# Stick-breaking attention, router constant, convolution taps and chunk scores of a two-layer decoder trunk in another order

## The chip, the core and the metric

The kernel runs on one core of one Trainium2 chip. A core has five engines with queues of their own: TensorE (PE, with its weight loads shown as PEld), VectorE (DVE), ScalarE (ACT), GpSimd (POOL) and SyncE (SP, which here only starts DMA transfers). An engine works through its queue in order and waits on semaphores of the others. The metric is the device time of one execution in microseconds (us); less is better.

## The reference, cut to what matters

Two layers over 256 tokens of width 1024, in fp32. Each layer is a mixer and a mixture of experts; a router common to both layers picks the experts. Layer 0's mixer runs a causal convolution of 31 taps (512 channels) beside stick-breaking attention (8 heads of 64); layer 1's runs chunked gated linear attention (4 heads) beside a pooling mixer.

```python
# stick_breaking_attention, for each block of 128 queries and the keys up to it
z = einsum('bhqd,bhkd->bhqk', q[:, :, start:end], k[:, :, :end])
strict = s_pos < t_pos
log_keep = where(strict, log_sigmoid(-z), 0.0)
later = cumsum(log_keep, axis=3, reverse=True) - log_keep
a = where(strict, exp(log_sigmoid(z) + later), 0.0)
outs.append(einsum('bhqk,bhkd->bhqd', a, v[:, :, :end]))
# gla_chunked
scores = where(causal, einsum('nbhid,nbhjd->nbhij', q_in, k_in), 0.0)
# before each mixture of experts
h = rmsnorm(x, norm_ffn[l]) * (1.0 + sc2) + sh2
scores = softmax(h @ router_w)
```

The router's logits are taken apart: `h @ router_w` is the token's norm times a product with `rwg` = router_w · norm_ffn · (1 + sc2), plus a row of 16 numbers that no token changes, sh2 @ router_w. That row is the **router's constant** `rc`.

## The kernel before, in words

Everything on the chip stays channel by token or token by channel in tiles of 128 partitions; weights come from HBM in a ring of 1 MB buffers, started by SP in program order as buffers come free. In the mixers each weight piece is split in two parts of reduced precision (`g`: L55 on ACT, L56 on DVE) and multiplied by both parts of the activations. The Python code is the order: each engine's queue holds its instructions in the order in which the code issues them, and generators (`next`, `conv`, `fill`) lay small pieces of one job between those of another.

**Layer 0, projections (56 to 105 us).** Five projections `pj` (L418, L423) of 512 columns each; the last three carry the convolution between their pieces by `conv(1 + k % 2, 1 + k % 2)`: so many taps of two generators.

- `taps` (L548) is DVE's share: 59 taps on `yc`, each `yc[k] += yp[k] shifted · weight` (L553; the first of a block L550). It takes channel block 2 (taps 0 to 15), then all 31 of block 0, then 12 of block 1.
- `other_taps` (L558) is the share of ACT and POOL: ACT multiplies (`cv`, L567, three buffers) and POOL adds (L568): block 3 whole, then block 2 from tap 16 on into the same `yc[:, 2]`, then block 1 from tap 12 on into `more`, added at the end (L570).

**Layer 0, attention (105 to 150 us).** Heads go in four pairs `cc`, the two heads of a pair in partitions 0 to 63 and 64 to 127 of `qT` and `kT`. For each pair: `logits` (L608, PE) makes z in PSUM, a product of `identb` and `maskb` putting the mask on its two diagonal blocks; `minus` and `softplus` (ACT and DVE, L624 to L634) make zs and ze; `sums` (L641 to L644, PE) the cumulative sums; `weights` (L648, L649 on DVE, the exp L650 on ACT) the attention weights; `attend` (L655, PE) the product with the values; `attended` (L666 ACT, L667 DVE) takes it out. The driver runs logits(0), logits(1), and then, in a loop over cc, sums(cc), logits(cc + 2), softplus(cc + 1), weights(cc), attend(cc). Between them stand taps (`conv(2, 3)`, `conv(3, 2)`) and, on PE, `fill(n)`: n groups of 8 records (`ada`, L190) of the conditioning product, which streams 1 MB tiles and is needed much later.

**Layer 0, output projection (150 to 200 us).** `po` (L453) in two halves, the second in four blocks i of 256 columns; after each, DVE updates `xT` (L481), and `norm.logits(i - 1)` (`lg`, L293) gives the router's logits of that block. Before the second half stands `Norm.weights` (L370): `gain` (L367), `rwg` (L374), the eight products of `rc` (L377) and its copy to SBUF. Layer 1 does the same (at 530 us).

**Layer 1's mixer (460 to 545 us).** Its projections are again pieces of `pj` on PE, between which steps of a generator lay the gated linear attention: `gs` (L923) are the scores within chunks, for row half q = 0, then 1; `kv` (L938) the products of keys and values.

**Experts (200 to 460 and 560 to 789 us).** Per expert `u`, `g` (L1252) and `dn` (L1285) from weights that stream through the same ring.

## Time and profile before

| what | value |
|---|---|
| median of 3 runs | 794.8 us (791.4, 794.8, 4035.95) |
| the profiled execution | 791.18 us, span 789.5 us |
| busy: PE, DVE, ACT, POOL | 93%, 40%, 30%, 15% of the span |
| mean granted TensorE clock | 0.977 |
| from HBM | 280.59 MB, 357 GB/s over the span |
| longest groups on PE | u and g (L1252) 225.7 us, dn (L1285) 101.7 us, pj 112.7 us, ada 52.0 us, po 51.1 us |

Times in the rows are us from the start of the span. A granted clock of 1.00 is TensorE's upper level of 2.4 GHz, 0.50 the lower of 1.2 GHz. The span says what can be won inside the program; 1.7 us of the profiled execution lie around it.

### The profile page before, as it was taken

The page shows a single profiled execution, that of the slowest core. Times are in us where ns is not written, and L with a number is a line of the kernel's source. Part 1 is how long each engine was busy: PE and PEld are TensorE (multiplying, and loading weights), DVE is VectorE, ACT ScalarE, POOL GpSimd, SP SyncE. Part 2 cuts the span into 40 slices and gives each one's busy share as a digit, 9 for nine tenths or more (in the row PEclk, how much of TensorE's full clock was granted, in tenths as well). Part 3 has the DMA queues.
Part 4 walks back from the last instruction along what each step waited for, and adds up shares of the span by engine and source line. Part 5 has one row for each costly group of instructions (what it writes and reads, how often), then busy time and mean ns, then how long its engine had stood idle before and what let it go on. Part 6 is the DMA issues. An engine that isn't in the chain of part 4 may idle for free. (4 is left out here: it accounts for less than half of the span.)

```text
span 789.5 us, 10674 instructions
## 1 busy us (share of the span) xinstructions
PE 730.9 (93%) x4173; PEld 402.8 (51%) x4173; DVE 313.8 (40%) x563; ACT 235.1 (30%) x441; POOL 120.0 (15%) x168
## 2 busy tenths in 40 slices
PE   6798888998899999999797999999999999999985
PEld 4398645486434335343233677579534334434323
DVE  3459968675214113121115655453513123213214
ACT  3357657463102101110113544551402101001012
POOL 1357646222000000000004500010300000000000
PEclk9999999999999999999999999999799999999999
DMA  8999739954999999999999998496699999999992
GB/s 357 386 375 419 291 121 398 372 219 183 351 410 409 409 409 409 409 408 409 409 405 391 396 414 322 171 402 235 255 385 412 408 409 409 409 408 409 408 403 106
DMA packets 74713, 282.46 MB, mean 358 GB/s; under 512 B 5194, under 2 KB 6438, under 8 KB 69530
## 3 DMA queue, kind: packets, MB, share of 16 engines
q1 hardware_dynamic: 73122, 278.68, 89.9%
q0 software_dynamic: 1344, 2.64, 0.9%
q8 instruction: 35, 0.57, 0.3%
q10 hardware_dynamic: 184, 0.34, 0.1%
q14 instruction: 28, 0.23, 0.1%
HBM read 280.59 MB, written 1.05 MB: 357 GB/s over the span
## 5 line engine op out<-in xcount | busy, mean ns | idle before, releaser
L1252 PE MATMUL g<-w,xg 128*64 128x512 f32 x512 | 115.0, 597 | 1.9 <-DMA w<-in_moe_w_gate_dram 1.8
L1252 PE MATMUL u<-w,xg 128*64 128x512 f32 x496 | 110.7, 594 | 2.1 <-DMA w<-in_moe_w_up_dram 2.1
L1285 PE MATMUL dn<-w,at 128*64 128x512 f32 x448 | 101.7, 604 | 8.1 <-ACTq L1383 6.8
L1264 DVE TENSOR_TENSOR act<-sg,u 128x512 f32<-128x512 f32 (+1 forms) x18 | 11.1, 628 | 153.0 <-PE u L1252 153.0
L1252 PEld LDWEIGHTS u<-w,xg 128*64 128x64 f32 x496 | 34.6, 137 | 72.1 <-issue 64.7
L1252 PEld LDWEIGHTS g<-w,xg 128*64 128x64 f32 x512 | 35.1, 137 | 68.6 <-issue 61.2
L56 DVE TENSOR_TENSOR g<-wi,g 128x512 fp32r<-128x512 f32 x72 | 58.1, 816 | 24.8 <-ACT g L55 24.6
L1285 PEld LDWEIGHTS dn<-w,at 128*64 128x64 f32 x448 | 31.1, 138 | 70.8 <-issue 56.8
L423 PE MATMUL pj<-hT,g 128*128 128x256 f32 x480 | 61.4, 285 | 6.0 <-DVE g L56 4.7
L423 PEld LDWEIGHTS pj<-hT,g 128*128 128x128 f32 x480 | 57.8, 188 | 10.0 <-DVE g L56 6.8
L418 PE MATMUL pj<-g,hT 128*128 128x512 f32 x192 | 51.3, 414 | 7.4 <-DVE g L56 3.5
L55 ACT ACTIVATE g<-wi 128x512 fp32r<-128x512 f32 x72 | 44.4, 626 | 39.1 <-PE pj L423 20.2
L190 PE MATMUL ada<-ad,cond 128*32 128x512 f32 x384 | 52.0, 653 | 4.0 <-DMA ad<-in_ada_w_dram 4.0
L453 PE MATMUL po<-cat,g 128*128 128x256 f32 x372 | 51.1, 290 | 2.5 <-ACT gsr L1006 1.7
L453 PEld LDWEIGHTS po<-cat,g 128*128 128x128 f32 x372 | 46.8, 196 | 6.7 <-ACT gsr L1006 2.6
L418 PEld LDWEIGHTS pj<-g,hT 128*128 128x128 f32 x192 | 35.4, 193 | 22.4 <-DVE g L56 6.7
L568 POOL TENSOR_TENSOR yc<-yc,cv 128x256 f32<-128x256 f32 x45 | 38.9, 864 | 22.8 <-ACT cv L567 20.0
L553 DVE SCALAR_TENSOR_TENSOR yc<-yp,epar,yc 128x256 f32<-128x256 f32 x56 | 41.3, 737 | 1.0
L1317 ACT ACTIVATE ys<-y 128x512 fp32r<-128x512 f32 x28 | 16.9, 625 | 67.1 <-DVE y L1307 62.3
L1275 DVE COPY at<-at 128x512 f32<-128x512 f32 x14 | 9.7, 692 | 67.5 <-PE at L1274 65.9
L1311 ACT ACTIVATE y<-dn,cw 128x512 f32<-128x512 f32 x7 | 4.8, 687 | 103.8 <-PE dn L1285 103.8
L1260 ACT ACTIVATE sg<-g 128x512 f32<-128x512 f32 x14 | 8.4, 597 | 89.4 <-PE g L1252 89.4
(385 smaller groups left out, 887.4 us busy)
## 6 DMA issues: line engine op xcount, KB each, us to landing
w<-in_moe_w_gate_dram SPq DMA_DIRECT2D x64, 1024.0 KB, 16.1
w<-in_moe_w_up_dram SPq DMA_DIRECT2D x62, 1024.0 KB, 18.3
w<-in_moe_w_down_dram SPq DMA_DIRECT2D x61, 1024.0 KB, 18.3
ad<-in_ada_w_dram SPq DMA_DIRECT2D x48, 1024.0 KB, 8.7
wi<-in_w_in_even_dram SPq DMA_DIRECT2D x20, 512.0 KB, 12.1
wi<-in_w_in_odd_dram SPq DMA_DIRECT2D x14, 512.0 KB, 12.5
wo<-in_w_out_even_dram SPq DMA_DIRECT2D x4, 1024.0 KB
wo<-in_w_out_odd_dram SPq DMA_DIRECT2D x4, 1024.0 KB, 18.6
```

The lines of the kernel that those rows point to most:

```text
L55: S.activation(g[0], w, AF.Copy)
L56: (eng or V).tensor_tensor(g[1], w, g[0].bitcast(F32), op=OP.subtract)
L190: PE.matmul(acc[32 * j:32 * j + 32, :], lhsT=cond[:, k, :], rhs=w[:, k - (i if n == 2 else 2 * i), c0:c0 + 512], start=i == 0, stop=i == 4 ...
L418: PE.matmul(bs[t], lhsT=self.h[j][:, k, t * 128:(t + 1) * 128], rhs=g[i], start=k == 0 and p == 0, stop=k == 7 and p == 2)
L423: PE.matmul(bs[c // 2][:, (c % 2) * T:(c % 2 + 1) * T], lhsT=g[i][:, c * 128:(c + 1) * 128], rhs=self.h[j][:, k, :], start=k == 0 and c % ...
L453: PE.matmul(self.acc[kd // 2][:, (kd % 2) * T:(kd % 2 + 1) * T], lhsT=block(g[wi], kd % 4), rhs=cats[ci][:, k, :], start=start and kd % 2 ...
L553: V.scalar_tensor_tensor(yc[:, k], yp[:, k, j:j + T], epar[:, k, j:j + 1], yc[:, k], op0=OP.mult, op1=OP.add)
L568: G.tensor_tensor(y, y, p, op=OP.add)
L1252: PE.matmul(b[64 * e:64 * e + 64, :], lhsT=xg[:, k, o + 64 * e:o + 64 * e + 64], rhs=we[:, e, k % 2 * 512:k % 2 * 512 + 512], start=k == 0 ...
L1264: V.tensor_tensor(a[:, n], sg[:, n], ub[:, n], op=OP.mult)
L1285: PE.matmul(bs[h][64 * e:64 * e + 64, :], lhsT=at[k][:, 64 * e:64 * e + 64], rhs=r[:, e], start=k == 0, stop=k == 3)
L1317: S.activation(ys[:, 0, n], y[h], AF.Copy)
```

## The change

- `logits`: the four products of queries and keys of a pair come first, alternating between the heads; the first now covers 256 queries (two products before). The mask comes last, once per head over both diagonal blocks (twice per head before).
- `attend`: the products with the values alternate between the two heads (head 0 whole, then head 1 before).
- `gs`: the products of both row halves alternate in one group of eight (two groups of four before).
- router's constant: DVE multiplies router_w by sh2 (`rk`) and sums the eight values of a partition (`rp`, L379 of the new numbering); one product with `ones` on PE sums over partitions. It is issued behind `norm.logits(0)` of the second half of `po`; the eight products of before (L377) are gone.
- `taps`: DVE's taps go by turns over two lists, block 0, and block 2 followed by block 1; a tap is taken from the longer list.

```diff
--- before.py
+++ after.py
@@ -372,11 +372,17 @@
             self.gain()
             self.w = live.tile([128, 8, E], F32, tag="rwg", name=f"rwg{l}")
             V.tensor_tensor(self.w, rw, self.g[:, :, None].to_broadcast([128, 8, E]), op=OP.mult)
-            b = bank(f"rc{l}")
-            for k in range(8):
-                PE.matmul(b[:, 0:E], lhsT=mod[l][:, 3, k:k + 1].to_broadcast([128, 128]), rhs=rw[:, k, :],
-                          start=k == 0, stop=k == 7)
-            self.c = live.tile([128, E], F32, tag="rc", name=f"rc{l}")
+            by_k = live.tile([128, E, 8], F32, tag="arow", name=f"rk{l}")
+            V.tensor_tensor(by_k.rearrange("p e k -> p k e"), rw, mod[l][:, 3, :, None].to_broadcast([128, 8, E]), op=OP.mult)
+            of_p = live.tile([128, E], F32, tag="ap", name=f"rp{l}")
+            V.tensor_reduce(of_p, by_k, axis=AX.X, op=OP.add)
+            self.of_p = of_p
+
+        def constant(self):
+
+            b = bank(f"rc{self.l}")
+            PE.matmul(b[:, 0:E], lhsT=ones, rhs=self.of_p, start=True, stop=True)
+            self.c = live.tile([128, E], F32, tag="rc", name=f"rc{self.l}")
             S.activation(self.c, b[:, 0:E], AF.Copy)
 
         def shifted(self, k, out, f, eng):
@@ -485,6 +491,8 @@
                     fill(fills[i])
                     if i:
                         norm.logits(i - 1)
+                    if i == 1:
+                        norm.constant()
                     if i == 2:
                         norm.turned(0, self.banks)
             norm.tokens(0)
@@ -546,13 +554,17 @@
 
 
         def taps():
-            for k, n in ((2, 16), (0, 31), (1, 12)):
-                V.tensor_scalar(yc[:, k], yp[:, k, 0:T], epar[:, k, 0:1], epar[:, k, 31:32], op0=OP.mult, op1=OP.add)
-                yield
-                for j in range(1, n):
+
+            sums = [[(2, j) for j in range(16)] + [(1, j) for j in range(12)], [(0, j) for j in range(31)]]
+            while any(sums):
+                sums.sort(key=len)
+                k, j = sums[1].pop(0)
+                if j == 0:
+                    V.tensor_scalar(yc[:, k], yp[:, k, 0:T], epar[:, k, 0:1], epar[:, k, 31:32], op0=OP.mult, op1=OP.add)
+                else:
                     V.scalar_tensor_tensor(yc[:, k], yp[:, k, j:j + T], epar[:, k, j:j + 1], yc[:, k],
                                            op0=OP.mult, op1=OP.add)
-                    yield
+                yield
 
         def other_taps():
             more = pool.tile([128, T], F32, name="more")
@@ -608,14 +620,15 @@
         def logits(cc):
 
             z = zl[cc] = zz.tile([128, 2, 512], F32, tag="zz", name=f"z{cc}")
+            heads = [slice(64 * h2, 64 * h2 + 64) for h2 in range(2)]
+
+            for h2, r in enumerate(heads):
+                PE.matmul(z[:, h2, 0:256], lhsT=kT[r, cc, 0:128], rhs=qT[r, cc, :], start=True, stop=False)
+            for h2, r in enumerate(heads):
+                PE.matmul(z[:, h2, 256:384], lhsT=kT[r, cc, 128:256], rhs=qT[r, cc, 128:256], start=False, stop=False)
             for h2 in range(2):
-                r = slice(64 * h2, 64 * h2 + 64)
-                zh = z[:, h2]
-                PE.matmul(zh[:, 0:128], lhsT=identb, rhs=maskb, start=True, stop=False)
-                PE.matmul(zh[:, 0:128], lhsT=kT[r, cc, 0:128], rhs=qT[r, cc, 0:128], start=False, stop=False)
-                PE.matmul(zh[:, 128:256], lhsT=kT[r, cc, 0:128], rhs=qT[r, cc, 128:256], start=False, stop=False)
-                PE.matmul(zh[:, 256:384], lhsT=identb, rhs=maskb, start=False, stop=False)
-                PE.matmul(zh[:, 256:384], lhsT=kT[r, cc, 128:256], rhs=qT[r, cc, 128:256], start=False, stop=True)
+                PE.matmul(z[:, h2].rearrange("p (a t) -> p a t", a=2)[:, :, 0:128], lhsT=identb,
+                          rhs=maskb[:, None, :].to_broadcast([128, 2, 128]), start=False, stop=True)
 
 
         def minus(cc):
@@ -655,11 +668,12 @@
         def attend(cc):
             ob = zl[cc] = bank(f"att{cc}")
             a = zs[cc]
-            for h2 in range(2):
-                hc = slice((2 * cc + h2) * 64, (2 * cc + h2) * 64 + 64)
-                r = slice(64 * h2, 64 * h2 + 64)
-                PE.matmul(ob[r, 0:256], lhsT=vn[:, 0, hc], rhs=a[:, h2, 0:256], start=True, stop=False)
-                PE.matmul(ob[r, 128:256], lhsT=vn[:, 1, hc], rhs=a[:, h2, 256:384], start=False, stop=True)
+            for t in range(2):
+                for h2 in range(2):
+                    hc = slice((2 * cc + h2) * 64, (2 * cc + h2) * 64 + 64)
+                    r = slice(64 * h2, 64 * h2 + 64)
+                    PE.matmul(ob[r, 128 * t:256], lhsT=vn[:, t, hc], rhs=a[:, h2, 256 * t:256 + 128 * t],
+                              start=t == 0, stop=t == 1)
 
         def attended(cc):
             hi, lo = (c[:, 4 + cc, :] for c in cats)
@@ -914,18 +928,19 @@
             V.tensor_copy(kdn, halves(b))
             yield
 
-            for q in range(2):
-                b = bank(f"gs{q}").rearrange("p (c i) -> p c i", c=4)
-                o = slice(64 * q, 64 * q + 64)
-                for t in range(2):
-                    ts_ = slice(t * 128, t * 128 + 128)
-                    for cc in range(2):
+            bs = [bank(f"gs{q}").rearrange("p (c i) -> p c i", c=4) for q in range(2)]
+            for t in range(2):
+                ts_ = slice(t * 128, t * 128 + 128)
+                for cc in range(2):
+                    for q, b in enumerate(bs):
+                        o = slice(64 * q, 64 * q + 64)
                         PE.matmul(b[:, 2 * t + cc, :], lhsT=kT[o, cc, ts_], rhs=qT[o, cc, ts_], start=True, stop=True)
-                yield
+            yield
+            for q, b in enumerate(bs):
                 for t in range(2):
                     for cc in range(2):
                         V.copy_predicated(sc[:, t, 2 * cc + q], trii, b[:, 2 * t + cc, :])
-            yield
+                yield
             yield
 
             yield
```

**TensorE, the logits of the first head pair**, right behind the last piece of projection 4 (`z_1076`: the pair's PSUM tile). Before:

```order
L614 LDWEIGHTS identb
L614 MATMUL z_1076<-maskb,identb 128x128
L615 MATMUL z_1076<-qT,kT 128x128
L616 MATMUL z_1076<-qT,kT 128x128
L617 LDWEIGHTS identb
L617 MATMUL z_1076<-maskb,identb 128x128
L618 MATMUL z_1076<-qT,kT 128x128
```

These seven rows stand for one head and come again for the other. In the changed kernel the pair is:

```order
L626 MATMUL z_1076<-qT,kT 128x256 x2
L628 MATMUL z_1076<-qT,kT 128x128 x2
L630 LDWEIGHTS identb
L630 MATMUL z_1076<-maskb,identb 128x2x128
L630 LDWEIGHTS identb
L630 MATMUL z_1076<-maskb,identb 128x2x128
```

Fourteen rows became eight instructions, and the products of the two heads now stand next to each other.

**VectorE, the end of projection 4**: `g038` and `g039` are its last two weight pieces, `ze0` the first step of attention there. Before:

```order
L56 TENSOR_TENSOR g038_1014<-wi20484_981,g038_1014 128x512 [waits DMAHW1_49,Activation_49]
L553 SCALAR_TENSOR_TENSOR yc_276<-yp_153,epar_146,yc_276 128x256 [waits DVE_49]
L56 TENSOR_TENSOR g039_1027<-wi20484_981,g039_1027 128x512 [waits Activation_49]
L553 SCALAR_TENSOR_TENSOR yc_276<-yp_153,epar_146,yc_276 128x256 [waits DVE_49] x7
L626 SCALAR_TENSOR_TENSOR ze0_1114<-zs0_1112 128x768 [waits Activation_49]
```

And in the changed kernel:

```order
L56 TENSOR_TENSOR g038_1014<-wi20484_981,g038_1014 128x512 [waits DMAHW1_49,Activation_49]
L565 SCALAR_TENSOR_TENSOR yc_276<-yp_153,epar_146,yc_276 128x256
L56 TENSOR_TENSOR g039_1027<-wi20484_981,g039_1027 128x512 [waits Activation_49]
L565 SCALAR_TENSOR_TENSOR yc_276<-yp_153,epar_146,yc_276 128x256 [waits DVE_49]
L565 SCALAR_TENSOR_TENSOR yc_276<-yp_153,epar_146,yc_276 128x256
L565 SCALAR_TENSOR_TENSOR yc_276<-yp_153,epar_146,yc_276 128x256 [waits Pool_49]
L565 SCALAR_TENSOR_TENSOR yc_276<-yp_153,epar_146,yc_276 128x256 [waits DVE_49] x2
L563 TENSOR_SCALAR yc_276<-yp_153,epar_146 128x256
L565 SCALAR_TENSOR_TENSOR yc_276<-yp_153,epar_146,yc_276 128x256 [waits DVE_49]
L639 SCALAR_TENSOR_TENSOR ze0_1106<-zs0_1104 128x768 [waits Activation_49]
```

The number of taps is the same; a tap behind one of the other block has no wait for DVE itself, and the last tap of block 2 now stands here, behind a wait for POOL. POOL's first three additions into block 2 (`cv216` to `cv218`) are now these rows of its queue:

```order
L580 TENSOR_TENSOR yc_276<-yc_276,cv216_1038 128x256 [waits DVE_49,Activation_49]
L580 TENSOR_TENSOR yc_276<-yc_276,cv217_1041 128x256 [waits Activation_49,Pool_49]
L580 TENSOR_TENSOR yc_276<-yc_276,cv218_1051 128x256 [waits DVE_49,Activation_49]
```

The first waits for DVE's tap 14 of block 2, which now is the 33rd of DVE's 59 taps (before, block 2's sixteen came first of all); the third waits for tap 15, the last of block 2.

**TensorE, the router's constant of layer 0** (`po`: output projection, `acol`: a piece of the conditioning product). Before:

```order
L199 MATMUL acol_1624<-ident,arow_1444 128x128 x4
L377 MATMUL rc_1635<-rw,mod_148 128x16 x8
L453 MATMUL po_1450<-cat_1074,g_1551 128x256
L453 MATMUL po_1450<-cat_1075,g_1551 128x256
L453 MATMUL po_1450<-cat_1074,g_1551 128x256
```

In the changed kernel:

```order
L190 MATMUL ada_1651<-ad_1687,cond 32x512 x4
L293 MATMUL lg_1693<-rwg_1617,xT 128x16 x4
L384 MATMUL rc_1698<-rp_1621,ones 128x16
L459 MATMUL po_1436<-cat_1074,g_1595 128x256
L459 MATMUL po_1436<-cat_1075,g_1595 128x256
```

The eight products ahead of the second half of the output projection have become one, two blocks later; layer 1's rows read the same.

## Rows read from the trace of the kernel before

**Rows 1.** Busy time by stretch: us of each engine, PE clock, DMA share, GB/s.

```profile
106.00:138.00 32.00, 30.00 (x194) 16.59 (x195) 22.52 (x33) 23.29 (x43) 18.90 (x22) 0.95 0.78 306
460.00:545.00 85.00, 83.30 (x598) 63.19 (x597) 43.42 (x88) 39.43 (x84) 5.20 (x7) 1.00 0.85 328
...
183.00:190.00 7.00, 6.99 (x59) 6.90 (x58) 2.02 (x9) 1.04 (x3) 0.00 (x0) 0.95 0.05 17
```

**Rows 2.** Timeline of PE, one head's logits; columns start us, us, engine, line.

```profile
107.19 0.23 PE L614 MATMUL z<-maskb,identb 128*128 128x128 bf16 x1
107.35 0.49 PE L615 MATMUL z<-qT,kT 64*128 64x128 f32 x2
108.00 0.23 PE L617 MATMUL z<-maskb,identb 128*128 128x128 bf16 x1
108.57 0.23 PE L614 MATMUL z<-maskb,identb 128*128 128x128 bf16 x1
```

**Rows 3.** Busy time of two stretches, and PE's timeline, ada.

```profile
110.80:114.20 3.40, 3.40 (x16) 1.13 (x19) 2.40 (x5) 2.98 (x5) 0.64 (x1) 0.50 0.02 5
138.10:141.50 3.40, 3.40 (x14) 0.90 (x14) 3.29 (x6) 1.74 (x5) 3.08 (x5) 0.50 0.93 318
...
111.68 4.87 PE L190 MATMUL ada<-ad,cond 128*32 128x512 f32 x32
...
133.49 1.92 PE L190 MATMUL ada<-ad,cond 128*32 128x512 f32 x16
```

**Rows 4.** Timeline of PE, products of half the rows or columns.

```profile
122.05 0.66 PE L661 MATMUL att<-zs,vn 128*64 128x256 f32 x4
122.53 0.40 PE L662 MATMUL att<-zs,vn 128*64 128x128 f32 x4
...
481.25 1.16 PE L923 MATMUL gs<-gqT,gkT 64*128 64x128 f32 x8
...
491.97 1.09 PE L938 MATMUL kv<-gvn,gkdn 64*64 64x128 f32 x24
```

**Rows 5.** Page, DVE's taps; timelines of DVE, POOL and ACT, end of projection 4.

```profile
L553 DVE SCALAR_TENSOR_TENSOR yc<-yp,epar,yc 128x256 f32<-128x256 f32 x56 | 41.3, 737 | 1.0
...
101.29 1.21 DVE L56 TENSOR_TENSOR g<-wi,g 128x512 fp32r<-128x512 f32 x1
102.82 0.68 DVE L56 TENSOR_TENSOR g<-wi,g 128x512 fp32r<-128x512 f32 x1
...
93.35 8.60 POOL L568 TENSOR_TENSOR yc<-yc,cv 128x256 f32<-128x256 f32 x9
...
104.49 1.29 ACT L601 ACTIVATE vn<-pj 128x512 f32<-128x512 f32 x2 [4.89 <-PE pj L418]
```

**Rows 6.** Timelines of DVE, PE and ACT, the attention's steps.

```profile
112.36 0.96 DVE L634 SCALAR_TENSOR_TENSOR ze<-zs,ze 128x768 f32<-128x768 f32 x1 [0.96 <-ACT ze L631]
...
116.48 0.70 PE L641 MATMUL zc<-ze,later 128*128 128x256 f32 x2
...
119.56 0.84 ACT L650 ACTIVATE zs<-zs 128x768 f32<-128x768 f32 x1 [2.73 <-DVE zs L649]
128.29 0.84 ACT L650 ACTIVATE zs<-zs 128x768 f32<-128x768 f32 x1 [0.59 <-DVE zs L649]
...
130.27 0.66 PE L661 MATMUL att<-zs,vn 128*64 128x256 f32 x4
...
137.41 0.66 PE L661 MATMUL att<-zs,vn 128*64 128x256 f32 x4 [2.00 <-ACT zs L650]
```

**Rows 7.** Timelines of PE and DVE, the router's constant.

```profile
166.58 1.86 PE L377 MATMUL rc<-rw,mod 128*128 128x16 f32 x16
168.29 3.60 PE L453 MATMUL po<-cat,g 128*128 128x256 f32 x24
...
169.45 0.43 DVE L751 TENSOR_TENSOR cat<-yc,cat 128x256 fp32r<-128x256 f32 x1
...
531.55 1.96 PE L377 MATMUL rc<-rw,mod 128*128 128x16 f32 x16
```

## The prediction

> **What bounds the kernel now.** The busy time by stretch comes first, because the change touches four short stretches of a span of 789.5 us. In the attention (106 to 138 us) PE is busy 30.00 of 32 us and DVE and ACT 22.5 and 23.3; in layer 1's mixer PE is busy 83.30 of 85 us and DVE 43.42 [rows 1]. So in both an us less on PE's queue can be an us less of time, if what PE then meets is ready. In 183 to 190 us, ahead of layer 0's experts, PE is busy 6.99 of 7 us and the DMA share is 0.05 [rows 1]: the weights' ring is full and waits for PE. An earlier PE starts the transfers earlier too, and the experts move with it one to one.
>
> Next is PE's timeline of the logits. One head takes 1.38 us (107.19 to 108.57): 0.16 the first mask, 0.65 the two products of 128 columns behind it, 0.57 the second mask with its product [rows 2]. A pair takes 2.76. Then the steps of the attention, for what waits when PE comes sooner [rows 6], and the clock [rows 3].
>
> **The change part by part.**
>
> *Logits.* The nearest rows for products of 64 partitions that are not interrupted by masks are the scores of layer 1: 8 records (two for each product) in 1.16 us, 0.145 each [rows 4]. So 128 columns cost 0.29 and 256 columns 0.58. Whether the two heads run side by side no row shows for row halves alone. `kv`, on tiles of 64 rows and 64 columns in turn, takes 1.09 us for 24 records, 0.045 each, a third of a score's [rows 4]; the halves of the attended values, which differ in columns, overlap as well: the four records of L662 start 0.48 after the four of L661 that take 0.66 [rows 4]. I take them as side by side: 0.58 + 0.29 for both heads, and two masks of 0.16: 1.2 a pair, 1.56 saved, 6.2 for four. The other end is one after the other: 2 x 0.87 + 0.32 = 2.06, 0.70 saved, 2.8 for four.
>
> *What of it reaches the end.* sums(0) starts at 116.48; its ze was ready at 112.36 + 0.96 = 113.32 [rows 6]. Two pairs lie ahead of it, so it can move by 3.1 and comes just behind ze. exp(0), ended at 120.40, follows sums(0): 117.3. att(0), at 122.05 [rows 4], has three pairs ahead: minus 4.7 is 117.4, level with exp(0). Behind att(0) a chain takes over: its result leaves by ACT, on whose queue the next pair's softplus waits, then DVE, the weights and exp(1), which ended at 129.13, 7.08 after att(0) began [rows 6, 4]. That gives 124.45 now. att(1), with all four pairs ahead, could start at 130.27 - 6.2 = 124.1 and waits for exp(1): it moves by 5.8. att(2) waited 2.00 already and stands 7.14 behind att(1) [rows 6], by the same chain; so it and all behind it move by 5.8.
>
> Against that stands the clock. From 110.8 to 114.2 and from 138.1 to 141.5 TensorE's granted clock was 0.50, 1.2 GHz; the one came behind the logits, the other behind att(2)'s wait [rows 3, 6]. In the first, 32 records of ada took 4.87, where 16 take 1.92 at full clock: 1.03 lost [rows 3]. PE now waits at more places, and I count two more such stretches: 2.0. The attention gives **-3.8**, between -5.8 and, with six, about nothing.
>
> *Values.* The products of the two heads overlap before the change too [rows 4]: **0**. The Trainium skill, TensorE: Matmul & The Clock Gate, Part 3 on packing small matmuls, says that matmuls start and end strictly in program order. By it head 0's second product would hold back head 1's first, and alternation would gain; the trace speaks against it, since all four records of L661 stand ahead of those of L662 though the program has head 0's L662 before head 1's L661.
>
> *Taps.* DVE's taps are as many as before. Idle time ahead of them is 1.0 us in all [rows 5], so that taps of two blocks in turn can gain at most about that. What moves is tap 14 of block 2: POOL's first addition into that block now waits for it at the end of projection 4. POOL had added without pause (9 in 8.60 us), and while it is silent DVE is faster: a weight piece took 1.21 beside POOL and 0.68 alone [rows 5]. Some 2 us of DVE come back before the last piece g039, which ended at 103.50. But behind it stand now: two taps (1.0), POOL's two additions (1.9), and ACT's next multiplications, which wait for POOL's buffers and stand ahead of `vn` on ACT's queue. vn, at 104.49 [rows 5], came 1.0 behind g039, and the logits wait for it. So between 2 us sooner and 2.9 - 1 = 1.9 us later, the gain held to 0.8 by PE's own pieces of the projection. I take **0**.
>
> *Scores.* Two groups of 1.16 (the other reads the same as the one shown) become one, if halves run side by side: **-1.2**; if not, 0. PE sets the pace there [rows 1]; DVE's copies behind them have slack.
>
> *Router's constant.* Layer 1: 16 records in 1.96 [rows 7] go, two of 0.12 come: **-1.7**. Layer 0: PE would come 1.9 sooner to the second half of the projection, but its 24 records from 168.29 already end late by waiting for DVE's L751, which ended at 169.88 [rows 7]. The 1.86 us taken away turn into a longer wait: nothing, and the new product costs **+0.25**. DVE's two small operations stand behind `rwg` and ahead of xT's first update, whose product on PE comes behind the projection's next block of 24 records, over 3 us of PE's work [rows 7]. An estimate of half a us for both (the smallest subtraction of 128x256 there takes 0.43) lies beside that; if that cover were gone, 0.5 a layer.
>
> Sum: -3.8 + 0 + 0 - 1.2 - 1.7 + 0.25 = -6.4. The profiled execution took 791.2, so 784.8. The two undisturbed runs shown (791.4, 794.8) and this one have a mean 1.3 above it; with that, **786**. Two per cent is 16 us here, about what a measurement tells from no change.
>
> **The rivals.**
>
> *Row halves don't run side by side.* No row shows it directly. Then four pairs save 2.8, the scores nothing, the router's 1.45 stays, and no new wait arises: -4.2, **788**.
>
> *The attention is held by DVE and ACT.* They are busy 70% of that stretch [rows 1], and taps stand at fixed places between their steps; att(2)'s wait of 2.00 shows that chain. If it began at 105 us, not at att(0), PE's 6.2 us turn into waits: -1.2 - 1.45 = -2.65, **790**.
>
> *All of it comes through.* No further half-clock stretch, taps at their good end: -5.8 - 0.8 - 1.2 - 1.45 = -9.3, **783**.
>
> *Values gain too.* If the heads of a pair did not overlap before, three of the four products with values, on the chain of 7.1, would give up half of their 0.9 us, and the last as much: 4 x 0.45 = 1.8, **784**. This is what the rule of the Trainium skill cited above would do. The records of L661 and L662 speak against it.
>
> *Slower: the clock.* Each wait that PE gets (sums(0), att(0), att(1), the output projection at 168, layer 1's) is followed by 3.4 us at 1.2 GHz, as at 138.1 [rows 3]. A whole stretch at half clock loses 1.7. Gains without the clock are 8.45, so from five stretches on it decides; with six it is +1.8, **794**, against 792.5. For it: two stretches stand in the attention already. Against: att(1) and the logits at 118 us follow short waits or none, and the clock stayed whole. The Trainium skill, same page, Part 1, HAM oscillation, describes this: idle time between bursts lets the clock fall, and the next burst pays. The rows of 138.1 agree.
>
> **How the numbers follow.** Forecast 0.45 (786), halves apart 0.10, DVE and ACT 0.15, all through 0.13, values 0.05, clock 0.12. All but the last are gains under 16 us, so the change is the same within 2% at 0.95; 0.03 for faster, if waits elsewhere vanish as well, and 0.02 for slower, for the clock with the late vn. The range takes in all cases and, below, a cleaner passage (-13), above the clock with part of vn's 1.9: **779 to 795**.
>
> **What would show it.** Logits: a pair in 1.2 us on PE's timeline (2.0 if apart). The chain: sums(0) near 113.4, att(0) near 117.4, att(1) near 124.5, with waits on ACT's exp ahead of them; att(1) at 130 would mean that nothing came through. Clock: the number of 0.50 stretches between 105 and 200. Taps: vn near 104.5, DVE's tap of block 2 behind POOL. Scores: one group of 16 records in 1.2. Router: PE waiting about 1.7 longer near 168, and no wait at 531. I am wrong if the experts of layer 0 do not start sooner by what PE gained at 190, or if a stage that the change doesn't touch moves.

## The result, and the profile after

The changed kernel takes 785.38 us (median of 6 runs, 782.88 to 788.99) where the kernel before takes 793.46: a ratio of 0.9892, with a 95% interval of 0.986 to 0.9924, or 8.5 us. One of the six runs of the kernel before took 4035.95 us; it stands in that median and not in the ratio. The forecast was 786 within 779 to 795. The profiled execution has a span of 781.2 us, 8.3 under the one of before. Its line of the page, and the busy time by stretch, which answer to [rows 1] and [rows 3] (columns: us, busy time of PE, PEld, DVE, ACT and POOL, PE clock, DMA share, GB/s):

```profile
span 781.2 us, 10574 instructions
```

```profile
106.00:138.00 32.00, 26.44 (x178) 11.78 (x177) 27.83 (x38) 25.20 (x48) 24.10 (x27) 0.95 0.86 340
...
104.00:118.00 14.00, 11.95 (x98) 5.79 (x102) 11.52 (x15) 11.23 (x20) 9.93 (x11) 1.00 0.70 274
133.30:136.70 3.40, 3.40 (x17) 0.59 (x16) 3.24 (x6) 0.94 (x3) 3.04 (x4) 0.51 0.66 275
163.40:167.00 3.60, 3.52 (x15) 3.23 (x15) 3.53 (x7) 0.81 (x3) 1.91 (x2) 0.58 0.15 32
```

The stretch from 104 to 118 us in the kernel before:

```profile
104.00:118.00 14.00, 13.31 (x76) 7.23 (x76) 8.56 (x13) 9.55 (x16) 6.36 (x8) 0.88 0.47 157
```

PE is busy 26.44 us of the attention's stretch (106 to 138 us), 3.6 less than before, and waits more; DVE, which came to its work sooner, is busy 27.83 instead of 22.52. The clock is whole from 104 to 118 us (0.88 in that stretch before). Two stretches shown stand at 1.2 GHz: one behind the wait for the values of pair 2, as before, and a new one that begins at 164.

PE's timeline of the first two pairs' logits and of the attention's steps answers to [rows 2], [rows 4] and [rows 6]:

```profile
103.95 0.70 PE L626 MATMUL z<-qT,kT 64*128 64x256 f32 x4 [2.10 <-ACT vn L613]
104.49 0.39 PE L628 MATMUL z<-qT,kT 64*128 64x128 f32 x4
104.81 0.39 PE L630 MATMUL z<-maskb,identb 128*128 128x256 bf16 x2
105.13 0.70 PE L626 MATMUL z<-qT,kT 64*128 64x256 f32 x4
...
106.31 3.64 PE L190 MATMUL ada<-ad,cond 128*32 128x512 f32 x32
111.76 0.70 PE L654 MATMUL zc<-ze,later 128*128 128x256 f32 x2 [1.81 <-DVE ze L647]
...
116.17 0.87 PE L675 MATMUL att<-zs,vn 128*64 128x256 f32 x8 [0.24 <-ACT zs L663]
116.97 1.92 PE L190 MATMUL ada<-ad,cond 128*32 128x512 f32 x16
...
123.67 0.87 PE L675 MATMUL att<-zs,vn 128*64 128x256 f32 x8 [0.68 <-ACT zs L663]
125.35 0.74 PE L199 MATMUL acol<-ident,arow 128*128 128x128 f32 x4 [0.81 <-ACT arow L195]
...
131.69 0.87 PE L675 MATMUL att<-zs,vn 128*64 128x256 f32 x8 [2.02 <-ACT zs L663]
```

A pair starts 1.18 us behind the other (103.95 to 105.13) instead of 2.76, and 32 records of ada take 3.64 instead of 4.87. The values' 8 records, one group now, end 0.80 behind their start (116.17 to 116.97 where the next group starts); before it was 122.05 to 122.85, the same. PE now waits for vn (2.10), for DVE's ze (1.81), for ACT's exp (0.24, 0.68 and 2.02), and, newly, 0.81 at 125.35 for ACT's `arow`.

The output projection, and the scores of layer 1, answer to [rows 7] and [rows 4]:

```profile
160.44 1.61 PE L459 MATMUL po<-cat,g 128*128 128x256 f32 x9
163.42 3.79 PE L459 MATMUL po<-cat,g 128*128 128x256 f32 x15 [1.37 <-DVE cat L764]
167.14 1.15 PE L190 MATMUL ada<-ad,cond 128*32 128x512 f32 x8
...
173.22 0.37 PE L384 MATMUL rc<-rp,ones 128*128 128x16 f32 x2
...
477.86 1.16 PE L937 MATMUL gs<-gqT,gkT 64*128 64x128 f32 x16
...
526.87 0.63 PE L459 MATMUL po<-cat,g 128*128 128x256 f32 x3
```

The wait for DVE's L764 (L751 before) is 1.37 us, and the 15 records behind it take 3.79 us where 24 take 3.16 at full clock. The scores are one group of 16 records in 1.16 us. In layer 1 the output projection's second half starts at 526.87, right behind ada, where `rc` stood.

Where the 8.3 us of the two spans come from, by the start of the same PE work in both traces (change less before):

| first record of | before | shift in the change | what lies between |
|---|---|---|---|
| projection 4, 88.6 us | 88.61 | -1.2 | nothing that the change touches |
| logits(0) | 105.83 | -1.9 | taps, vn |
| att(1) | 130.27 | -6.6 | logits, clock at 111 to 114 |
| po, first half | 151.95 | -6.1 | ACT's queue behind exp(1) |
| lg(0), layer 0 | 176.90 | -4.6 | rc of layer 0, clock at 164 |
| gs | 481.25 | -3.4 | route, experts: 3.4 us more at 1.2 GHz near 430 |
| kv | 491.97 | -4.7 | scores |
| lg(0), layer 1 | 540.29 | -6.4 | rc of layer 1 |
| acc, layer 1's experts | 561.23 | -7.9 | 3.4 us less at 1.2 GHz near 550 |
| end | 789.5 | -8.3 | |

Most of the first row is there at 33 us (-1.3), before any changed instruction runs, and the twelve traces of the experiments show it too, from -0.2 to -1.7: the profiled execution of before began slowly.

### The profile page after: what moved, and what is told of

The parts are those of the page before. It is cut to its first block, busy times and chain, and to the rows that moved or that the text cites. A ratio compares the mean times of both kernels' runs of the same rounds, so it can differ in the third digit from the quotient of the medians.

```text
span 781.2 us, 10574 instructions
## 1 busy us (share of the span) xinstructions
PE 717.0 (92%) x4121; PEld 393.3 (50%) x4121; DVE 314.9 (40%) x567; ACT 235.0 (30%) x441; POOL 120.8 (15%) x168
## 5 line engine op out<-in xcount | busy, mean ns | idle before, releaser
L459 PE MATMUL po<-cat,g 128*128 128x256 f32 x372 | 52.9, 296 | 3.9 <-ACT gsr L1021 1.7
L190 PE MATMUL ada<-ad,cond 128*32 128x512 f32 x384 | 50.1, 630 | 4.9 <-DMA ad<-in_ada_w_dram 4.9
```

What stands on the lines that cost most here:

```text
L190: PE.matmul(acc[32 * j:32 * j + 32, :], lhsT=cond[:, k, :], rhs=w[:, k - (i if n == 2 else 2 * i), c0:c0 + 512], start=i == 0, stop=i == 4 ...
L459: PE.matmul(self.acc[kd // 2][:, (kd % 2) * T:(kd % 2 + 1) * T], lhsT=block(g[wi], kd % 4), rhs=cats[ci][:, k, :], start=start and kd % 2 ...
```

## The experiments

Each run is compared with the kernel before that ran beside it on the same chip; ratios have 95% intervals. Shifts are those of the traces, as in the table above; "net of the start" means less the shift that the trace already has at projection 4.

**The logits alone.** The kernel before with the new `logits` and nothing else (the hunk of `logits` in the diff above).

> The kernel before with the new logits alone (products of both heads in turn, mask last). Theory (PE's queue shortened, then a chain of 7.1 us from one pair's values to the next): a pair of logits in about 1.2 us on PE instead of 2.76; sums(0) about 3 us sooner than in the kernel before, the values of pair 1 and all behind them about 5 to 6 us sooner, no new stretch at 1.2 GHz in the attention; whole time 5 to 6 us under before (ratio about 0.993). Rival 1 (the clock takes part of it, as the prediction had it): one or two more stretches at 1.2 GHz between 105 and 150 us, 3.8 us under before. Rival 2 (the new order of the taps made room for it): only 3 us under before without it.

Ratio 0.9929 (0.99 to 0.9958), 790.3 us against 795.5. Its steps of the attention:

```profile
104.75 0.70 PE L614 MATMUL z<-qT,kT 64*128 64x256 f32 x4 [0.69 <-ACT vn L601]
...
105.93 0.70 PE L614 MATMUL z<-qT,kT 64*128 64x256 f32 x4
...
111.38 0.70 PE L642 MATMUL zc<-ze,later 128*128 128x256 f32 x2 [0.64 <-DVE ze L635]
...
115.79 0.66 PE L662 MATMUL att<-zs,vn 128*64 128x256 f32 x4 [0.24 <-ACT zs L651]
```

Less the slow start (-1.1), sums(0) is 4.0 sooner, att(0) 5.2, att(1) 5.8, and from att(2) on 5.0: 0.8 is lost between att(1) and att(2). The theory's figures hold but for sums(0), which moved 4.0 and not 3; neither rival does: the clock was not lowered between 104 and 118 us, and the taps were not needed.

Where the 0.8 goes is seen on ACT, alike in this run and in the change. Before, ACT took out the values of pair 1 0.94 us behind att(1) (130.27):

```profile
131.21 0.39 ACT L666 ACTIVATE cat<-att 128x256 fp32r<-128x256 f32 x1 [0.20 <-PE att L662]
```

In the change it does so 1.53 behind att(1) (123.67), since att(1) now follows exp(1) at once and three multiplications and `arow` stand between the two on ACT's queue:

```profile
123.53 1.29 ACT L579 ACTIVATE cv<-yp,epar 128x256 f32<-128x256 f32 x3
124.72 0.57 ACT L195 ACTIVATE arow<-ada 128x512 f32<-128x512 f32 x1
125.20 0.36 ACT L680 ACTIVATE cat<-att 128x256 fp32r<-128x256 f32 x1
```

DVE's steps for pair 2 follow from there:

```profile
126.30 1.26 DVE L639 SCALAR_TENSOR_TENSOR ze<-zs 128x768 f32<-128x768 f32 x1 [0.28 <-ACT zs L637]
127.49 2.35 DVE L565 SCALAR_TENSOR_TENSOR yc<-yp,epar,yc 128x256 f32<-128x256 f32 x3
129.75 0.68 DVE L661 TENSOR_TENSOR zs<-zs,zc 128x512 f32<-128x512 f32 x1
```

The first took 0.96 before. The last needs PE's sums(2), which had ended by 127.9; it starts behind the taps without a wait. So PE's own wait of 0.81 for `arow` at 125 us costs att(2) nothing: 0.59 of the delay is ACT's queue and 0.3 is ze on DVE.

**The taps alone.** The kernel before with the new `taps`.

> The kernel before with the new order of DVE's taps alone. Theory (DVE runs faster while POOL waits, and vn comes late for the same wait, so that the two nearly cancel): the projections' last product about 2 us sooner, the first product of the logits 0.5 to 1 us sooner, PE waiting about 2 us for vn; the whole time within 1 us of before. Rival (the late vn costs more): logits 1 us or more later than before and the whole time 1 to 2 us longer. Other rival (taps that alternate run faster by themselves): DVE's taps shorter beside POOL too, the projections 2 us or more shorter, and no loss behind them.

Ratio 1.001 (0.9978 to 1.0041). The projections and the logits:

```profile
103.96 0.22 PE L618 MATMUL z<-maskb,identb 128*128 128x128 bf16 x1 [2.09 <-ACT vn L605]
...
113.17 5.89 PE L190 MATMUL ada<-ad,cond 128*32 128x512 f32 x32
118.99 0.70 PE L645 MATMUL zc<-ze,later 128*128 128x256 f32 x2
```

PE waits 2.09 for vn (0.69 before: the projections end sooner than vn); the logits start 0.7 sooner, net of the start. So far the theory. Then comes what neither had: the clock is at 0.50 from 104 to 118 us, the first pairs take 4.6 us each, and sums(0) is 2.5 us later than in the kernel before. No instruction of this stretch differs from before but for DVE's taps; the next run, which has the old taps, shows a like stretch, so that the new taps are not needed for it.

**The router's constant alone.** The hunks of `weights`, `constant` and its call.

> The kernel before with the new router's constant alone. Theory: in layer 1 the output projection starts 1.8 us sooner; in layer 0 PE only comes sooner to its wait for DVE's last part of the concatenation (L751 of before), and the longer wait puts TensorE at 1.2 GHz for 3.4 us behind it, so that layer 0's router logits come 1.0 to 1.7 us later than in the kernel before; the whole time about 0.3 us under before. Rival (that stretch at 1.2 GHz came by chance of timing in the changed kernel, not from the wait): clock whole between 163 and 175 us, layer 0 about level, whole time 1.5 us under before.

Ratio 0.995 (0.9919 to 0.9981). In its trace layer 0's lg(0) keeps the attention's shift (2.67 at the projection, 2.68 at lg): nothing won, nothing lost. The wait ahead is 1.37, as in the change, but the 15 records behind it take 2.42, at full clock:

```profile
169.18 1.60 PE L459 MATMUL po<-cat,g 128*128 128x256 f32 x9
172.15 2.42 PE L459 MATMUL po<-cat,g 128*128 128x256 f32 x15 [1.37 <-DVE cat L758]
```

Layer 1's output projection comes 1.8 sooner (4.22 to 2.44); the ratio's 4 us are more than this trace accounts for. So the rival holds for this run: the wait need not lower the clock. Before the router's code runs at all, at 107 to 118 us, this kernel's clock was 0.50 too, with the logits of before.

**Scores and values alone.** The hunks of `attend` and `gs`.

> The kernel before with the new order of the values' products (attention) and of the scores (layer 1's mixer) alone. Theory: the eight records of a pair's values take 0.80 us in either order, so nothing moves in layer 0; the scores take one group of 1.16 us instead of two, so that kv comes 1.2 to 1.3 us sooner; whole time 1.2 us under before. Rival (matmuls start and end strictly in program order, so that only the new order lets two heads overlap): the values of a pair take 0.4 us less than before, layer 0 another 1 to 1.8 us sooner, whole time 2.5 to 3 us under before.

Ratio 0.9934 (0.9909 to 0.9959); the trace accounts for 1.3 us of it by the change (kv's shift goes from 0.02 to -1.28 at the scores; at att(0) and behind att(3) it stands at 0.16 and 0.12). A pair's values take 0.80 us as before:

```profile
130.43 0.87 PE L662 MATMUL att<-zs,vn 128*64 128x256 f32 x8
131.23 0.75 PE L199 MATMUL acol<-ident,arow 128*128 128x128 f32 x4
```

The rival falls. The Trainium skill's rule of TensorE: Matmul & The Clock Gate, Part 3 on packing small matmuls, that matmuls start and end strictly in program order, is not borne out for the starts: in the kernel before, head 1's records of L661 start ahead of head 0's of L662 [rows 4], and putting them in that order gains nothing here. (Their ends are modelled in the profile and say nothing.) Of the ratio's other 4 us the clock is a part: over the timed executions it was 0.978 here and 0.974 in the kernel before, by an estimate (that share of the span) 3 us; the profiled ones have 26.8 and 37.0 us at 0.50.

The four ratios of the parts alone come to 14 us together, the change to 8.5. They share one set of runs of the kernel before, and each is uncertain by 2 to 3 us, so that what a part is worth is better read from the traces.

**Head by head, masks last.** Does the alternation let the halves run side by side?

```diff
 for h2, r in enumerate(heads):
     PE.matmul(z[:, h2, 0:256], lhsT=kT[r, cc, 0:128], rhs=qT[r, cc, :], ...)
-for h2, r in enumerate(heads):
     PE.matmul(z[:, h2, 256:384], lhsT=kT[r, cc, 128:256], rhs=qT[r, cc, 128:256], ...)
```

> The changed kernel, but a pair's products of queries and keys go head by head (head 0's two, then head 1's two) instead of in turn; masks last as in the change, same number of products. Theory (the alternation lets the two row halves run side by side): a pair takes about 2.0 us instead of 1.18, the values of pair 1 come 1 to 2.5 us later than in the changed kernel, and the whole time is 1 to 3 us above the changed kernel's. Rival (halves overlap whenever the next product in the queue uses the other half, so that the gain came from the mask's two products in place of four and from fewer switches): a pair in 1.2 to 1.5 us, the whole time level with the changed kernel's within 1 us.

784.67 us, ratio 0.9867 (0.9836 to 0.9899): level with the change. A pair of logits:

```profile
104.28 0.71 PE L626 MATMUL z<-qT,kT 64*128 64x256 f32 x4 [2.09 <-ACT vn L613]
104.82 0.39 PE L627 MATMUL z<-qT,kT 64*128 64x128 f32 x4
105.15 0.39 PE L629 MATMUL z<-maskb,identb 128*128 128x256 bf16 x2
105.47 1.23 PE L626 MATMUL z<-qT,kT 64*128 64x256 f32 x4
```

From 104.28 to 105.47 it is 1.19 us. Records of both heads stand together although the program has both products of head 0 first: their starts are 13 ns apart (7 in the change). The theory falls: the order within the pair is not what counts. The rival's pair and time hold; whether fewer mask products paid, as it says, the run of four masks tells.

**A mask between the heads.** The same, with each head's mask right behind its products.

```diff
-for h2 in range(2):
-    PE.matmul(z[:, h2]..., lhsT=identb, rhs=maskb..., start=False, stop=True)
+    # inside the loop over heads, behind the head's two products
+    PE.matmul(z[:, h2]..., lhsT=identb, rhs=maskb..., start=False, stop=True)
```

> The changed kernel, but a pair's logits go head by head with the mask of each head right behind its two products, so that a product on 128 rows stands between the two heads. The run with the products head by head and both masks last was level with the change (a pair in 1.19 us), so the alternation itself is not what paid. Theory (the heads overlap because nothing on 128 rows stands between their products): here they cannot, and a pair takes 2 x (0.58 + 0.29 + 0.16) = 2.0 us or a little more; values of pair 1 come 1 to 3 us later than in the changed kernel, whole time 1 to 3 us above it. Rival (the two masks saved and the switches paid, overlap or not): a pair in 1.2 to 1.5 us and the time level with the changed kernel's.

788.42 us, ratio 0.9939 (0.9914 to 0.9963), 3 to 4 us above the change. At full clock:

```profile
118.15 0.70 PE L626 MATMUL z<-qT,kT 64*128 64x256 f32 x2
118.69 0.38 PE L627 MATMUL z<-qT,kT 64*128 64x128 f32 x2
119.00 0.28 PE L628 MATMUL z<-maskb,identb 128*128 128x256 bf16 x1
119.22 0.70 PE L626 MATMUL z<-qT,kT 64*128 64x256 f32 x2
...
120.28 1.07 PE L190 MATMUL ada<-ad,cond 128*32 128x512 f32 x8
```

A pair takes 2.13 us (118.15 to 120.28). So the two heads' being neighbours with no product on 128 rows between is worth 0.95 a pair; each head's products and masks merged, and its mask put last, are the other 0.63 of 2.76. The theory holds for the pair, and its times fall short: the values of pair 1 come 5.3 us later than in the change, not 1 to 3. sums(0) is 4.5 us later than in the change, of which two pairs explain 1.9; the rest goes with the clock, at 0.50 from 104 to 114 us, as with the old logits.

**Four masks.** The change with each head's mask in two products of 128 columns, behind all products.

```diff
-PE.matmul(z[:, h2]...[:, :, 0:128], lhsT=identb, rhs=maskb[:, None, :].to_broadcast([128, 2, 128]), ...)
+PE.matmul(z[:, h2, 0:128], lhsT=identb, rhs=maskb, start=False, stop=False)
+PE.matmul(z[:, h2, 256:384], lhsT=identb, rhs=maskb, start=False, stop=True)
```

> The changed kernel, but each head's mask in two products of 128 columns as before the change, still behind all products of queries and keys. Theory (columns and switches count, not the number of mask products): the four masks take 0.32 to 0.45 us together instead of 0.32 for two, a pair 1.2 to 1.3 us, the time level with the changed kernel's. Rival (each mask product costs its 0.16 us as before the change): a pair in 1.5 us, up to 1.2 us more over four pairs.

785.2 us, ratio 0.9888 (0.9857 to 0.992): level. The pair takes 1.18 us, the four masks start within 0.17 us of each other. The theory holds; merging the masks paid nothing, and by the run before, keeping them together did.

**An earlier ada.** Work for PE where it waits in the output projection.

```diff
 n01.weights()
-po.second(((), (2, 3, 0, 1)), [c[:, 0:4] for c in cats], n01, (1, 1, 0, 0))
+fill(1)
+po.second(((), (2, 3, 0, 1)), [c[:, 0:4] for c in cats], n01, (0, 1, 0, 0))
```

> The changed kernel, but 8 records of ada (0.96 us of PE work that stood behind the first block of the output projection's second half) are issued ahead of that half, where PE waits 1.37 us for DVE. Theory (the wait makes the stretch at 1.2 GHz): the wait falls to about 0.4 us, the clock stays whole between 163 and 167 us, layer 0's router logits come 1.0 (work moved into the wait) + 1.5 (clock) = 2.5 us sooner than in the changed kernel; whole time about 2.5 us under it. Rival (the clock falls there for what came before, not for the wait): still 3.4 us at 0.50, only 1.0 us sooner. Second rival (DVE sets the end of that block): nothing.

782.43 us, ratio 0.9851 (0.9814 to 0.9888): lower than the change's, with intervals that overlap.

```profile
160.44 1.06 PE L190 MATMUL ada<-ad,cond 128*32 128x512 f32 x8
161.43 1.35 PE L459 MATMUL po<-cat,g 128*128 128x256 f32 x9
163.26 5.31 PE L459 MATMUL po<-cat,g 128*128 128x256 f32 x39 [0.47 <-DVE cat L764]
```

The wait is 0.47, the clock whole, and lg(0) 2.8 us sooner than in the change: 1.2 by the trace's own shifts from the projection to lg (-6.24 to -7.41), the rest, but for 0.2, the stretch at 1.2 GHz that isn't there. That the wait shrinks and the work moves into it is shown; whether the wait made the stretch needed the repeat below.

**vn ahead.** ACT's last two multiplications of projection 4 move behind the values' evacuation, and the next four behind the first softplus.

```diff
-project(4, ..., step=lambda k: conv(1 + k % 2, 1 + k % 2))
+project(4, ..., step=lambda k: conv(1 + k % 2, (1 + k % 2) * (k < 7)))
 logits(1)
-conv(2, 4)
+conv(2, 0)
 minus(0)
 softplus(0)
-conv(2, 0)
+conv(2, 2)
 ...
-conv(2, 2)
+conv(2, 4)
```

> The changed kernel, but ACT's last two multiplications for POOL's share of the convolution no longer stand ahead of vn, and the four that stood ahead of the first pair's softplus stand behind it (POOL's work is the same, later). Theory (in the changed kernel the late vn and those four multiplications, which wait for POOL, hold sums(0)): PE's wait of 2.10 us for vn falls to about 1, its wait of 1.81 us ahead of sums(0) goes for the most part, the values of all pairs come 1.5 to 2.5 us sooner; whole time 1.5 to 2.5 us under the changed kernel. Rival (POOL's later work then holds the group norm behind the attention, which needs the last addition): the values come sooner, but the second group norm does not, and the whole time is level within 0.5 us.

788.8 us, ratio 0.9923 (0.9897 to 0.995): some 2 to 3 us above the change by the ratios, and 4 above the kernel with the products head by head that ran beside it. The wait for vn falls to 0.69 and sums(0) comes 2.8 sooner than in the change, but att(0) only 0.5, since ACT's multiplications now stand ahead of its exp. Two of POOL's additions were left for the end, and there PE pays:

```profile
143.74 2.04 PE L686 MATMUL gm<-yc,bones 128*128 128x512 f32 x2 [4.32 <-DVE yc L582]
```

4.32 us of waiting for DVE's last addition L582, 0.76 in the change. On DVE it waits for POOL:

```profile
143.17 0.43 DVE L582 TENSOR_TENSOR yc<-yc,more 128x256 f32<-128x256 f32 x1 [1.84 <-POOL more L580]
```

The rival's wait is there, and the whole time comes out worse than it said.

**Both.** The two edits before this one together (the earlier ada, vn ahead).

> The two edits before this one together, on the changed kernel. Theory: their gains add, 4 to 5 us under the changed kernel, about 780 us where the changed kernel takes 785. Rival (PE comes to the second half of the output projection sooner, DVE does not): the gain of the attention turns into a longer wait at 160 us, and only that of the earlier ada, 1 to 2.5 us, is left.

782.17 us, ratio 0.9841 (0.9808 to 0.9874), level with the earlier ada alone. The attention's end came 1.4 us later than in the change (wait for the last addition 2.75), lg(0) 1.3 sooner. The gains don't add; as the end of the attention is late with vn ahead alone, this says nothing on the rival.

**The earlier ada with the old taps.**

> The changed kernel with the 8 records of ada ahead of the output projection's second half, and with DVE's taps in the order of the kernel before. Theory (the new order of the taps gives 0.6 us at the logits and takes as much ahead of sums(0), where ACT's multiplications wait for POOL): the values of pairs 1 and 2 come 0 to 0.5 us sooner than with the new taps, whole time level with or 0.5 us under that kernel's, 2 to 3 us under the changed kernel's. Rival (the new taps are worth their 0.6 us): 0.6 us above the kernel with the earlier ada alone.

784.26 us, ratio 0.9895 (0.9863 to 0.9927). Net of the start, logits(0) has no shift (-0.7 with the new taps), sums(0) is 4.0 sooner (3.5 with the new ones), att(1) 5.8 (5.4): what the new taps win ahead of the logits they lose ahead of sums(0), and 0.4 more, as the theory had it. The whole time is level with the change's, not 2 to 3 us under it as the theory said. The time between the two orders is not settled: this trace has 9.4 us more at 1.2 GHz than that of the earlier ada, 6.8 of them in the attention.

**The change once more.**

> The changed kernel once more, as it is. It tells two things apart. Of the stretch at 1.2 GHz from 163 to 167 us: if the wait of 1.37 us ahead of it makes it, it is there again, and layer 0's router logits come 1.5 us later against the attention's values than in the kernel before; if it is a matter of the moment (it was missing with the router's constant alone and with the products head by head, and there with vn ahead, all with the same wait), it may be missing, and they come level. Of the attention's clock: in four kernels with the old logits the clock was 0.50 for 3.4 to 13 us between 104 and 118 us, in six with the new logits for 0 to 3.4 us; here at most 3.4 us is expected. Whole time 783 to 787 us.

784.27 us, ratio 0.9883 (0.9859 to 0.9907).

```profile
160.68 1.60 PE L459 MATMUL po<-cat,g 128*128 128x256 f32 x9
163.65 2.42 PE L459 MATMUL po<-cat,g 128*128 128x256 f32 x15 [1.37 <-DVE cat L764]
```

The same wait of 1.37, and full clock behind it: 15 records in 2.42. lg(0) keeps the shift of the projection (-5.82 at both). So this wait alone does not settle whether the stretch at 164 comes. In seven traces with this wait it is there in four (the change, vn ahead, the mask between, four masks) and costs 1.4 to 1.5 us each; with ada in the wait it is in none of three, too few to tell that from chance.

**The clock in the logits, over all traces.** Us at 1.2 GHz between 102 and 121 us:

| logits of | kernels | us at 1.2 GHz |
|---|---|---|
| one head at a time, between products on 128 rows | before, taps, router, scores and values, mask between | 3.4, 13.7, 10.2, 6.8, 10.2 |
| both heads together | change, change again, logits, head by head, four masks | 0, 3.4, 0, 3.4, 0 |
| both heads together, other edits | earlier ada, vn ahead, both, old taps | 0, 3.4, 3.4, 0 |

The busy time from 104 to 118 us with the mask between the heads:

```profile
104.00:118.00 14.00, 14.00 (x60) 7.05 (x59) 7.53 (x9) 8.41 (x14) 7.70 (x10) 0.63 0.31 96
```

PE is busy all 14 us and its clock is 0.63; in the change it was busy 11.95 at 1.00, as shown above. DMA has a share of 0.31 against 0.70; the records of ada, whose tiles it refills, end at 116 us there and at 110 in the change. So the logits' form goes with the clock in 14 traces; what in it lowers the clock no run shows. In the two longest cases (taps, mask between) the clock fell at 104 us, right behind the wait of 2.1 for vn. In the change's second trace it fell soon behind the same wait too, at 105.5, but for 3.4 us only. What sets the old logits apart is above all how long it stayed low.

Over whole spans the difference is small. The mean granted clock of the timed executions is 0.974 with one head at a time (88 executions) and 0.976 with both together (55), by an estimate (that share of the span) 2 us; single kernels scatter as much (scores and values 0.978, head by head 0.974). The change's repeat and the kernel before that ran beside it have 0.9765 and 0.9757.

## Why the prediction was right, and where not

- **Logits.** 1.2 us a pair was forecast, 1.18 measured. (The sum as the prediction writes it reads 0.58 for both heads and two masks of 0.16, which is 0.90; it comes out at 1.2 with the head's second product, 0.58 + 0.29 = 0.87, as in its other end.) The reason given was half right: the heads do run side by side, as the forecast took them to, but not by the alternation that the change put in (head by head is level) and not by fewer masks (four are level). What paid most is that no product on 128 rows stands between them.
- **The step that failed: the clock.** The forecast took 2.0 us off the attention for two more stretches at 1.2 GHz between 105 and 150 us, where the kernel before has 6.8 us. None came in the change, and the one at 111 us went; the nine traces with the new logits have 0 to 6.8 there. What the clock gave back on ada's 32 records (4.87 to 3.64) did not reach sums(0): PE waited 1.81 for ze instead. With the old logits the clock can cost more: in the run of the taps PE took 15.0 us from the first logits to sums(0), for work of 2 x 2.76 + 3.64 = 9.2 at full clock.
- **The chain.** att(1) moved by 5.8 in the run of the logits alone, the forecast's figure, but by two misses that cancel. The forecast left ze at its old time; it moves with its logits, so that sums(0) came 4.0 sooner and not 3.1, and att(0) 5.2 and not 4.7. And the chain from att(0) to att(1) was 7.6 and not 7.08: DVE's ze in it took 1.15 instead of 0.96, and two taps ahead of that 1.83 instead of 1.00. "att(2) stands 7.14 behind att(1)" became 8.0: ACT's queue behind exp(1), which had been free in time before, now stands in the chain, as shown above. In all the attention of the change gave 4.9 net of the start; 3.8 was the forecast, from -5.8 and +2.0.
- **Taps.** 0 forecast; 0.7 sooner at the logits, and by att(1) 0.4 later than with the old taps. The forecast weighed the late vn; it left out that four more of ACT's multiplications, paced by POOL, stand ahead of the first softplus.
- **Values.** 0, as forecast: the eight records of a pair take 0.80 us in either order.
- **Scores.** -1.2 forecast, -1.3 measured.
- **Router.** -1.7 forecast for layer 1, -1.7 in the change's trace (kv to lg) and -1.7 alone. Layer 0: +0.25 forecast, 0.0 measured in three traces at full clock, +1.4 to +1.5 in four with the stretch at 164, the change's profile among them.
- **Sum.** By place, the change's trace gives -4.9 + 1.5 - 1.3 - 1.7 = -6.4, the forecast's figure. That it agrees is in part chance: the attention gave 1.1 more and layer 0's projection 1.2 less. The change's second trace, without the stretch at 164, gives -4.9 + 0 - 1.3 - 1.7 = -7.9. The other -1.9 of the first trace's span are the start (-1.2) and stretches of the clock in the experts and ahead of layer 1's, which no part of the change explains. A stage that the change doesn't touch thus did move, one of the prediction's own signs of being wrong; that twelve other traces start sooner too puts it down to the profile of before.

Open stays why the clock falls behind a wait in one execution and not in the next, and what in the old logits keeps it low. The ratio's 8.5 us lie closer to the second trace's 7.9 than to the forecast's 6.4; the clock over whole spans, level between the two kernels, does not account for the difference.

## What to carry to other kernels

Products on half the rows of TensorE should stand next to those on the other half, with every product on all rows outside: the order within the group is free, and one product between the halves cost 0.95 us a pair. An us taken from a busy engine's queue is worth something only up to the next wait: follow each step to what it waits for, and then look again at what stands ahead of that step on its own engine, since work that was done in time before (here ACT's multiplications and `arow` behind exp(1)) can now lie in the chain. A wait that the profile shows, as PE's 0.81 for `arow`, need not cost anything. Where PE must wait, work without a due time put into the wait saves its own length (1.2 to 1.3 us in each of three traces), and in those three the clock stayed whole behind it.

## What the runs showed of the hardware that was not expected

Products of two row halves start 13 ns apart even if the program has them in sequence of 2 and 2. Stretches at 1.2 GHz lay at partly other places in the two profiled executions of the change, and their sum differed: 30.1 us in one trace and 33.5 in the other, of 781 and 784.
